# Tokens as the stationary operand for sixteen columns, and a rearranged hand-over to the last stage

## The chip, the cores and the metric

The kernel runs on one core of one Trainium2 chip. The metric is device time in microseconds (us), the median of several executions; here three executions of the kernel before gave 1936.08, 1943.45 and 1945.98 us. One further execution was recorded by the hardware profiler, and all views of the trace come from that one.

The engines of a core run side by side, each through its own list of instructions in order: PE multiplies matrices, DVE (VectorE) and ACT (ScalarE) do elementwise work and read PSUM, where PE leaves its results, POOL (GpSimd) does elementwise work on SBUF alone, and SP issues the transfers.

## The reference

One layer of a hybrid encoder, over 2048 prompt tokens and 32 sample tokens of width 1024:

```
h = layer_norm(x, ln0_g, ln0_b)
qa, ka, va, za, qkv_b, zb, a_b, b_b, gate_a, gate_b = split(h @ w_in)   # 6160 columns; a_b, b_b have 8 each
oa = chunk_band_attention(qa, ka, va, rel_bias)                  # branch A
q, k, v = silu(causal_conv(qkv_b, conv_w))                       # branch B
g    = -exp(a_log) * softplus(a_b + dt_bias)                     # decay
beta = sigmoid(b_b)
ob = rms_norm(gated_delta_rule(q, k, v, g, beta))
ya = (oa * silu(za)) @ w_branch_a;  yb = (ob * silu(zb)) @ w_branch_b
mix = sigmoid(gate_a) * ya + sigmoid(gate_b) * yb
y = layer_norm(ALPHA * h + mix @ w_out, ln_g, ln_b)              # ALPHA = 2 ** 0.25
```

## The kernel before, in words

**Stages.** The tokens go in two halves (1024, and 1024 + 32). For each half a phase B (delta rule) and then a phase A (attention) run, and under both, all the time, the input projection: 48 jobs of 128 columns of `w_in` and one job "ab" with the 8 + 8 columns of decay and beta. Sixteen jobs of a half are the merge gates; they feed nothing in the phases and serve as filling for PE. When phase A of the second half ends, the last stage ("merge") multiplies the mixed branches by `w_out`, adds the residual, normalises and stores.

**A job.** `fetch` loads 128 columns into one of two places `wraw`; `divide` finds their scale in the first half (ACT squares and sums them, PE sums over the partitions with a matmul by the tile `tiny`, `power` turns the sum into a power of two on DVE, POOL and DVE), scales them on ACT and splits them into two f16 parts, `whi` by ACT and `wlo` by POOL. `multiply` runs blocks of up to 512 tokens. Weights are the stationary operand, tokens (`hi`, `lo`, the two f16 parts of h) the moving one, so a block of 512 tokens is 8 x 3 matmuls of 128x512 into one of two PSUM banks `pj`. The job ab puts its columns' low parts beside the high ones in the same 128 columns of `whi`, and so needs 8 x 2 matmuls a block; ACT reads one group of result rows, DVE adds the other, and tokens lie along the free dimension from the start.

**The order of the work.** `Flow` is a planner that runs while the program is built: every step is a small generator, it is given a time by assumed prices, and instructions are recorded in the order of these times. All instructions of an engine thus stand in one fixed list. `HEAD` and `TAIL` are the numbers of gate jobs per half ahead of the job ab, and between the phase-B jobs and the phase-A jobs; what is left of the sixteen comes after the phase-A jobs. Since the recording goes through one helper, nearly every instruction has line L276 in the profile; L301 is a plain transfer, L312 a transposing one.

**The hand-over to the merge.** `early` multiplies the branch outputs (`ghi`, `glo`) by `w_a` or `w_b` ahead of the merge and stores the products (`sg`, later `sl`) in the buffers `sig` in DRAM. In the merge, `load` brings two of them back as `sf`, `fold` adds them (DVE) and rounds them on ACT to `mh`, the rest being `ml`. `w_out` has eight row blocks k = 0 to 7; `load_o` loads k = 0 to 3 through the places `wraw` into the space that the tokens had, after both `h_free` gates are open, that is after the last job's first and last block. Then the front space is given free (`front_done`) and `last_weights` loads the rows `l0g` and `l0b`, multiplies both by ALPHA on ACT, then loads k = 4 to 7 as halves `wr` and `lnb`. `x_ahead` loads the inputs again as `xt` and rebuilds the residual from them with `l0g` and `l0b`.

## Time and profile before

| what | value |
|---|---|
| median of three executions | 1943.45 us (1936.08 to 1945.98) |
| the profiled execution, its own time | 1944.59 us |
| its span, first to last instruction | 1942.5 us |
| granted TensorE clock, mean | 0.987 |
| PE busy | 1863.8 us, 96% |
| DVE, ACT, POOL busy | 1392.5, 987.7, 812.0 us |
| moved by transfers | 274.51 MB, 141 GB/s over the span |

A busy PE is the union of its matmuls' modelled times, and matmuls overlap; what one costs in a stream is the distance from start to start, which the timeline gives. In the timeline, the columns are start, duration, engine, line, operation and its operands, and in brackets the idle time just before it with what ended it. Landmarks of the span: the first attention scores of the first half start at 533.9 us, the job ab of the second half at 798.0, the last scores at 1657.9, the merge at 1698.6.

### The profile page before, as it was taken

How to read it: one execution, taken by the hardware profiler on the slowest of the kernel's cores; microseconds unless marked ns; L12 is line 12 of the kernel's file. 1: busy time of each engine (PE TensorE's matmuls, PEld its weight loads, DVE VectorE, ACT ScalarE, POOL GpSimd, SP SyncE). 2: the span in 40 equal slices, each digit the busy share in tenths (PEclk: the TensorE clock that was granted, in tenths of full speed). 3: DMA queues.
4: the chain of work that ended last, by engine and by line, in shares of the span. 5: the costliest groups of instructions: out<-in, count | busy, mean ns of one | idle time of the engine just before them, and what ended most of it. 6: DMA issues, size and time to landing. Idle time of an engine off the chain costs nothing.

```text
span 1942.5 us, 39504 instructions
## 1 busy us (share of the span) xinstructions
PE 1863.8 (96%) x13812; PEld 1296.6 (67%) x13812; DVE 1392.5 (72%) x4248; ACT 987.7 (51%) x2010; POOL 812.0 (42%) x1165
## 2 busy tenths in 40 slices
PE   8999999999999999999999999999999999899998
PEld 5445666767454556666778768767778667678886
DVE  7689997973377778679998986365456565475797
ACT  6665545444486878564545443355446574321110
POOL 7354445443443435355344443423222242253673
PEclk8999999999999999999999999999999999999999
DMA  3224342242468887222233242478778798995552
GB/s 134 72 90 111 78 110 80 76 110 82 124 160 188 186 188 176 68 82 71 67 96 103 61 109 72 134 209 207 215 181 200 180 200 202 260 329 190 182 184 88
DMA packets 382943, 274.51 MB, mean 141 GB/s; under 512 B 248338, under 2 KB 319358, under 8 KB 382744
## 3 DMA queue, kind: packets, MB, share of 16 engines
q1 hardware_dynamic: 382744, 272.00, 52.7%
q8 instruction: 108, 1.77, 0.4%
q14 instruction: 91, 0.75, 0.1%
HBM read 157.15 MB, written 71.76 MB: 118 GB/s over the span
## 4 chain that ended last, share of the span: by engine, by line
PE 67%; DVE 18%; issue 4%; DMA 4%; ACT 4%; POOL 2%; SPq 1%; POOLq 0%; DVEq 0%; ACTq 0%
PE pj L276 39%; PE b L276 10%; PE a L276 6%; DVE sys_u L276 4%; PE x L276 3%; PE c L276 3%; DVE acc L276 2%; PE d L276 2%; PE o L276 2%; DVE sys_t L276 2%; POOL wlo L276 1%; DVE v_t L276 1%; SPq L301 1%; DVE st L276 1%; ACT whi L276 1%
## 5 line engine op out<-in xcount | busy, mean ns | idle before, releaser
L276 PE MATMUL pj<-hi,whi 128*128 128x512 f16 (+2 forms) x1992 | 644.6, 339 | 10.1 <-ACT part L276 2.3
L276 PE MATMUL pj<-hi,wlo 128*128 128x512 f16 (+2 forms) x1952 | 636.4, 339 | 1.1 <-POOL wlo L276 1.0
L276 PEld LDWEIGHTS <-whi 128*128 128x128 f16 x3984 | 404.5, 103 | 241.9 <-issue 14.9
L276 PE MATMUL pj<-lo,whi 128*128 128x512 f16 (+2 forms) x1992 | 449.5, 338 | 0.0
L276 POOL TENSOR_TENSOR wlo<-wraw,whi 128x256 f16<-128x256 f32 (+1 forms) x392 | 281.8, 741 | 360.8 <-ACT whi L276 321.6
L276 PEld LDWEIGHTS <-wlo 128*128 128x128 f16 x1952 | 200.8, 103 | 129.0 <-issue 16.6
L276 POOL TENSOR_TENSOR pu<-sb,pu 128x640 f16<-128x640 f32 (+2 forms) x64 | 81.8, 1278 | 177.8 <-ACT pu L276 142.2
L276 ACT ACTIVATE wraw<-wraw,w_scale 128x1024 f32<-128x1024 f32 (+1 forms) x98 | 111.3, 1136 | 73.2 <-DVE w_scale L276 70.8
L276 ACT CAST whi<-wraw 128x512 f16<-128x512 f32 (+2 forms) x212 | 128.0, 611 | 38.4 <-PE pj L276 35.2
L276 ACT ACTIVATE sb<-sb,mx,unit 128x640 f32<-128x640 f32 (+4 forms) x128 | 108.6, 849 | 69.5 <-DVE mx L276 63.3
L276 DVE SCALAR_TENSOR_TENSOR acc<-raw,cwT,acc 128x512 f32<-128x512 f32 x144 | 112.9, 784 | 8.8 <-ACT acc L276 7.6
L276 ACT CAST mh<-sf 128x256 fp32r<-128x256 f32 x64 | 25.6, 406 | 153.3 <-PE c L276 80.5
L276 DVE CUSTOM_DVE_ANT_0 sb<-a,bias 128x320 f32<-128x320 f32 (+5 forms) x136 | 66.5, 498 | 44.9 <-PE a L276 39.9
L276 DVE SCALAR_TENSOR_TENSOR sys_u<-sys_p,sys_u 128x20 f32<-128x20 f32 (+11 forms) x408 | 93.4, 275 | 3.7 <-DMA sys_p<-sol_p 1.4
L276 POOL TENSOR_TENSOR ml<-sf,mh 128x256 fp32r<-128x256 f32 x60 | 62.1, 1036 | 81.0 <-PE c L276 43.7
L276 POOL TENSOR_TENSOR st<-state,sc 128x128 f32<-128x128 f32 (+1 forms) x80 | 31.1, 388 | 142.6 <-DVE state L276 122.7
L276 DVE TENSOR_TENSOR sys_u<-sys_u,sys_t 128x60 f32<-128x60 f32 (+17 forms) x323 | 79.2, 246 | 5.7
L276 DVE SCALAR_TENSOR_TENSOR sg<-sg,b 128x512 f32<-128x512 f32 (+2 forms) x49 | 29.7, 606 | 74.5 <-PE b L276 66.1
L276 ACT CAST pu<-sb 128x640 f16<-128x640 f32 (+4 forms) x128 | 82.3, 650 | 1.4 <-DMA pt<-pu 0.8
L276 ACT ACTIVATE sig<-pj,w_both 128x512 f32<-128x512 f32 (+2 forms) x84 | 49.2, 586 | 66.2 <-PE pj L276 54.2
L276 DVE TENSOR_TENSOR sys_t<-sys_u,sys_p 128x60 f32<-128x60 f32 (+17 forms) x323 | 78.6, 244 | 5.6
L276 PEld LDWEIGHTS <-pt 128*128 128x128 f16 x1680 | 65.7, 98 | 22.6 <-issue 3.7
(390 smaller groups left out, 4045.3 us busy)
## 6 DMA issues: line engine op xcount, KB each, us to landing
wraw<-in_w_in SPq DMA_DIRECT2D x192, 256.0 KB
sf<-sig SPq DMA_DIRECT2D x112, 128.0 KB
sig<-sig SPq DMA_DIRECT2D x44, 256.0 KB
sg<-sig SPq DMA_DIRECT2D x40, 256.0 KB
sig<-sg SPq DMA_DIRECT2D x40, 256.0 KB
sys_p<-sol_p SPq DMA_DIRECT2D x68, 128.0 KB
x<-in_x_p SPq DMA_DIRECT2D x16, 512.0 KB
xt<-in_x_p SPq DMA_DIRECT2D x16, 512.0 KB
```

The lines of the kernel that those rows point to most:

```text
L276: r = f(*a, **k)
L301: eng.dma_start(dst, src)
```

## The change

1. **Job ab with tokens stationary.** The sixteen columns are loaded as one piece. `whi` holds 16 high and 16 low columns, and they move past the tokens: for each 128 tokens and each k, one matmul with `hi` stationary and 32 moving columns, and one with `lo` stationary and 16. The results have tokens on the partitions. ACT reads the low group of a block, DVE adds the high group into a tile `abt`, PE transposes it 128 tokens at a time into a bank `b`, and DVE and ACT go on from there as before.
2. **ScalarE reads the sums.** In `power`, for all but the first four jobs, the step that takes the sum out of PSUM and adds 1e-24 is an ACT instruction in place of a DVE one (45 times).
3. **One gate job moved.** `TAIL` goes from [6, 5] to [5, 5]: in the first half one gate job stands after the phase-A jobs and no longer ahead of them.
4. **Residual unscaled.** `l0g` and `l0b` are not multiplied by ALPHA any more (two ACT instructions of 128x1024 less). The product's factor becomes 0.5 / ALPHA, and LN_EPS is divided by ALPHA squared, which gives the same normalised rows.
5. **First quarter of w_out sooner.** `load_o` takes k = 0 and 1 once the first gate `h_free` is open, and k = 2 and 3 once the second is.

```diff
-HEAD, TAIL = [2, 3], [6, 5]
+HEAD, TAIL = [2, 3], [5, 5]
...
-        V.tensor_scalar(out=out, in0=ps[:, 0:1], scalar1=1e-24, scalar2=None, op0=ALU.add)
+        if len(started) > 4:
+            S.activation(out=out, in_=ps[:, 0:1], func=AF.Copy, bias=1e-24)
+        else:
+            V.tensor_scalar(out=out, in0=ps[:, 0:1], scalar1=1e-24, scalar2=None, op0=ALU.add)
...
-        for g in h_free:
-            yield g
         for i in range(2):
+            yield h_free[i]
...
-        for k in range(KO):
-            yield from load_rows(w_out, k, lambda c: [x[k][:, c * 512:(c + 1) * 512] for x in wo],
-                                 lambda c: w_ready["o", k, c])
+            for k in range(2 * i, 2 * i + 2):
+                yield from load_rows(w_out, k, lambda c, k=k: [x[k][:, c * 512:(c + 1) * 512] for x in wo],
+                                     lambda c, k=k: w_ready["o", k, c])
...
+                if job.cols < P:
...
+                    for i in range(len(tiles)):
+                        m, W = min(P, n - i * P), job.cols
+                        toks = slice(i * P, i * P + m)
+                        for k in range(KD):
+                            PE.matmul(ps[:m, i * 2 * W:(i + 1) * 2 * W], hh[:, k, toks], wh[:, k, 0:2 * W],
+                                      start=(k == 0), stop=False)
+                            PE.matmul(ps[:m, i * 2 * W:i * 2 * W + W], hl[:, k, toks], wh[:, k, 0:W],
+                                      start=False, stop=(k == KD - 1))
...
-                S.activation(out=ab[0:40], in_=ps[HD:HD + 40, 0:n], func=AF.Copy, scale=inv[HD:HD + 40])
+                V.memset(rows, 0.0)
+                S.activation(out=halves, in_=lo_, func=AF.Copy, scale=inv)
                 yield
-                V.scalar_tensor_tensor(out=ab[0:40], in0=ps[0:40, 0:n], scalar=inv[0:40], in1=ab[0:40], op0=ALU.mult,
-                                       op1=ALU.add)
+                V.scalar_tensor_tensor(out=halves, in0=hi_, scalar=inv, in1=halves, op0=ALU.mult, op1=ALU.add)
                 bank["pj"].give()
                 yield
-                V.tensor_scalar(out=ab[0:NH], in0=ab[0:NH], scalar1=dtb[:], scalar2=None, op0=ALU.add)
-                S.activation(out=ab[32:40], in_=ab[32:40], func=AF.Tanh, scale=0.5)
+                yield bank["b"]
+                ps = pt("b")
+                for i in range(nt):
+                    PE.transpose(ps[0:40, i * P:i * P + m], rows[:, i, 0:40], ident[:m, :m])
+                yield
+                V.tensor_scalar(out=ab[0:NH], in0=ps[0:NH, 0:n], scalar1=dtb[:], scalar2=None, op0=ALU.add)
+                S.activation(out=ab[32:40], in_=ps[32:40, 0:n], func=AF.Tanh, scale=0.5)
+                bank["b"].give()
...
-            S.activation(out=r, in_=r, func=AF.Copy, scale=ALPHA)
...
-            V.scalar_tensor_tensor(out=xt[:rows, cs], in0=part, scalar=0.5, in1=xt[:rows, cs],
+            V.scalar_tensor_tensor(out=xt[:rows, cs], in0=part, scalar=0.5 / ALPHA, in1=xt[:rows, cs],
```

**How the order moves.** Three places show it; names are those of the program, with the buffers' numbers partly left out.

PE, second half, the end of the job ab and the first matmuls of the next job. Before:

```order
L276 LDWEIGHTS whi
L276 MATMUL pj<-lo_9305,whi 128x32
L276 LDWEIGHTS whi
L276 MATMUL pj<-lo_9305,whi 128x32
L276 LDWEIGHTS whi
L276 MATMUL pj<-hi_9018,whi 128x512
L276 LDWEIGHTS wlo
L276 MATMUL pj<-hi_9018,wlo 128x512
L276 LDWEIGHTS whi
```

After:

```order
L276 LDWEIGHTS lo_9437
L276 MATMUL pj<-whi,lo_9437 32x16
L276 LDWEIGHTS hi_9436
L276 MATMUL pj<-whi,hi_9436 32x32
L276 LDWEIGHTS lo_9437
L276 MATMUL pj<-whi,lo_9437 32x16
L276 MATMUL b<-ident,abt 40x128 x8
L276 LDWEIGHTS whi
L276 MATMUL pj<-hi_9221,whi 128x512
```

The job now ends with 32-token blocks whose stationary operand is the tokens, and the eight transposes of its two 512-token blocks stand ahead of the next job's first matmul. They read `abt`, which ACT and DVE write from PSUM first.

ACT, first half, one weight job between the squares (`whi,w_sq<-wraw`) and the scaling (`wraw<-wraw,w_scale`). Before:

```order
L276 ACTIVATE whi,w_sq<-wraw_145 128x1024
L276 ACTIVATE sig<-pj,w_both 128x512
L276 COPY u_bd_747<-tu 32x8x32 x4
L276 ACTIVATE wraw_145<-wraw_145,w_scale 128x1024
L276 CAST whi<-wraw_145 128x512
L276 COPY z_c<-d 32x256 x2
```

After:

```order
L276 ACTIVATE whi,w_sq<-wraw_145 128x1024
L276 ACTIVATE sig<-pj,w_both 128x512
L276 COPY v_t_765<-o 128x64
L276 COPY v_t_763<-o 128x64
L276 ACTIVATE w_scale<-b 128x1
L276 ACTIVATE wraw_145<-wraw_145,w_scale 128x1024
```

The reading of the sum, `w_scale<-b`, stands on ACT's own list now, ahead of the scaling.

SP, around the start of the merge: `wraw<-in_w_out` are two of the row blocks k = 0 to 3, `l0g` the first row of `last_weights`, `sf` the merge's first operands, `glo`, `sl` and `sg` the operands and results of `early`. Before, the last of k = 0 to 3, then the merge's first transfers:

```order
L301 DMA wraw_146<-in_w_out 128x1024
L301 DMA ga_15851<-za_91 128x256
L301 DMA sig_71<-sg 128x512
L301 DMA g_66<-ga_15850 128x256
L301 DMA sig_72<-sg 128x512
L301 DMA sg<-sig_74 128x512
L301 DMA sig_73<-sg 128x512
L301 DMA g_66<-ga_15851 128x256
L301 DMA sg<-sig_75 128x512
L301 DMA l0g<-in_ln_g 128x1024
L301 DMA sf<-sig_68 128x256
L301 DMA sf<-sig_76 128x256
```

After, the merge's first transfer, and then the place where k = 2 and 3 stand:

```order
L301 DMA sig_73<-sg 128x512
L301 DMA sg<-sig_75 128x512
L301 DMA g_66<-ga_16109 128x256
L301 DMA sig_74<-sig 128x272
L301 DMA sf<-sig_68 128x256
L301 DMA sf<-sig_76 128x256
```

```order
L301 DMA glo<-g_66 128x4x256 x2
L301 DMA sl<-sig_68 128x512
L301 DMA sl<-sig_69 128x512
L301 DMA sl<-sig_70 128x512
L301 DMA sl<-sig_71 128x512
L301 DMA sl<-sig_72 128x512
L301 DMA sl<-sig_73 128x512
L301 DMA sig_75<-sg 128x512
L301 DMA wraw_145<-in_w_out 128x1024
L301 DMA wraw_146<-in_w_out 128x1024
L301 DMA sig_75<-sig 128x272
```

Before, k = 0 to 3 all stand ahead of the first `sf`, with `l0g` between. Now k = 0 and 1 stand 26 rows ahead of it, k = 2 and 3 stand 19 rows behind it, `l0g` 36 rows behind it, and the halves of k = 4 to 7 stand 44 to 77 rows behind it (12 to 35 before).

More of the change, by code (lines that the diff above doesn't have):

```diff
@@ L716, in divide @@
                 yield
-                rest_ = lo[:, ks] if job.cols == P else hi[:, ks, job.cols:P]
+                rest_ = lo[:, ks] if job.cols == P else hi[:, ks, job.cols:2 * job.cols]
                 for q in range(0, 4, 2):
@@ L762, in multiply @@
                 ps = pt("pj")
+                if job.cols < P:
+                    for i in tiles:
+                        yield l_ready[job.half][i]
+                    for i in range(len(tiles)):
[6 more added lines that the diff above has]
+                                      start=False, stop=(k == KD - 1))
+                            if k % 4 == 3:
+                                yield
+                    if bi == len(job.blocks) - 1 and not job.own:
+                        w_gate.give()
+                    flow.start(evac(job, bi, c0, n, gcol, ps))
+                    continue
                 for k in range(KD):
@@ L765, in multiply @@
                     yield
-                    if job.cols == P:
-                        PE.matmul(ps[:, 0:n], wl[:, k], hh[:, k, :], start=False, stop=False)
-                        yield
+                    PE.matmul(ps[:, 0:n], wl[:, k], hh[:, k, :], start=False, stop=False)
+                    yield
                 for i in tiles:
@@ L1002, in evac @@
                 ab = raw[:, c0:c0 + n] if bi < 2 else raw_s[:, 0:n]
-                inv = w_inv[:, 48:49]
-                S.activation(out=ab[0:40], in_=ps[HD:HD + 40, 0:n], func=AF.Copy, scale=inv[HD:HD + 40])
+                m, nt = min(n, P), (n + P - 1) // P
+                inv = w_inv[:m, 48:49]
+                rows = bp.tile([P, 8, 32], F32, tag=("tu", "tu_t", "z_c")[bi], bufs=1, name="abt")
+                rows = rows[:].rearrange("p (t a) r -> p t (a r)", a=2)[:m, 0:nt]
+                halves = rows.rearrange("p t (g r) -> p t g r", r=32)[:, :, :, 0:NH]
+                hi_, lo_ = (ps[:m, 0:nt * 32].rearrange("p (t w g r) -> w p t g r", w=2, g=2, r=NH)[w] for w in range(2))
+                V.memset(rows, 0.0)
+                S.activation(out=halves, in_=lo_, func=AF.Copy, scale=inv)
                 yield
-                V.scalar_tensor_tensor(out=ab[0:40], in0=ps[0:40, 0:n], scalar=inv[0:40], in1=ab[0:40], op0=ALU.mult,
-                                       op1=ALU.add)
+                V.scalar_tensor_tensor(out=halves, in0=hi_, scalar=inv, in1=halves, op0=ALU.mult, op1=ALU.add)
                 bank["pj"].give()
                 yield
-                V.tensor_scalar(out=ab[0:NH], in0=ab[0:NH], scalar1=dtb[:], scalar2=None, op0=ALU.add)
-                S.activation(out=ab[32:40], in_=ab[32:40], func=AF.Tanh, scale=0.5)
+                yield bank["b"]
+                ps = pt("b")
+                for i in range(nt):
+                    PE.transpose(ps[0:40, i * P:i * P + m], rows[:, i, 0:40], ident[:m, :m])
+                yield
+                V.tensor_scalar(out=ab[0:NH], in0=ps[0:NH, 0:n], scalar1=dtb[:], scalar2=None, op0=ALU.add)
+                S.activation(out=ab[32:40], in_=ps[32:40, 0:n], func=AF.Tanh, scale=0.5)
+                bank["b"].give()
                 yield
@@ L2139, in all_jobs @@
                 elif what == "ab":
-                    yield Job(half, 48, [(0, w_ab[:, :, 0:NH]), (32, w_ab[:, :, NH:2 * NH])], key=(1, None, 0), cols=HD,
-                              blocks=AB_BLOCKS[half])
+                    yield Job(half, 48, [(0, w_ab)], key=(1, None, 0), cols=2 * NH, blocks=AB_BLOCKS[half])
                 else:
@@ L2198, in row, with landed @@
             t = dma(rowv[name][:], src.rearrange("(o d) -> o d", o=1).to_broadcast([P, D]))
-            if name[0:2] == "l0":
-                flow.start(scale(rowv[name][:], t, name == "l0b"))
+            if name == "l0b":
+                flow.start(landed(t))
             yield t - LEAD
-        def scale(r, t, last):
+        def landed(t):
             yield t
-            S.activation(out=r, in_=r, func=AF.Copy, scale=ALPHA)
-            if last:
-                rows_ready.done()
+            rows_ready.done()
         for name, src in (("l0g", ln0_g), ("l0b", ln0_b)):
@@ L2501, in finish @@
         V.bn_aggr(out=m2[:rows], in_=w.st[:rows])
-        V.tensor_scalar(out=m2[:rows, 1:2], in0=m2[:rows, 1:2], scalar1=LN_EPS, scalar2=None, op0=ALU.add)
+        V.tensor_scalar(out=m2[:rows, 1:2], in0=m2[:rows, 1:2], scalar1=LN_EPS / ALPHA ** 2, scalar2=None, op0=ALU.add)
         yield
```

## The prediction

> **What bounds the kernel now.** I read the page first (share of each engine, then the forty slices), then the waits of PE, then PE's timeline at each place where the change touches it.
>
> ```profile
> PE 1863.8 (96%) x13812; PEld 1296.6 (67%) x13812; DVE 1392.5 (72%) x4248; ACT 987.7 (51%) x2010; POOL 812.0 (42%) x1165
> PE   8999999999999999999999999999999999899998
> ```
>
> PE is full in all slices, and no stage has another bound. So time is won only as PE work removed or PE waits removed; work of other engines counts only where PE waits for it. The largest single wait of PE, and those of the job ab:
>
> ```profile
> PE a L276 <- ACT mh L276: 8.0, 1, 8.0
> ...
> PE pj L276 <- DVE ab L276: 1.5, 1, 1.5
> ...
> PE b L276 <- DVE ab L276: 1.2, 1, 1.2
> ```
>
> The first is the hand-over to the merge. The many others are below 5 us in sum each.
>
> **Edit 1, job ab.** PE's timeline of the job in both halves (first row: its start; 65.30: the next job):
>
> ```profile
> 58.36 1.89 PE L276 MATMUL pj<-hi,whi 128*128 128x512 f16 x8
> ...
> 65.30 0.38 PE L276 MATMUL pj<-hi,whi 128*128 128x512 f16 x1
> ...
> 798.02 1.89 PE L276 MATMUL pj<-hi,whi 128*128 128x512 f16 x8
> ...
> 804.92 0.35 PE L276 MATMUL pj<-hi,whi 128*128 128x32 f16 x8
> 805.13 0.35 PE L276 MATMUL pj<-lo,whi 128*128 128x32 f16 x8
> 807.03 0.38 PE L276 MATMUL pj<-hi,whi 128*128 128x512 f16 x1 [1.55 <-DVE ab L276]
> ...
> 812.96 1.13 PE L276 MATMUL b<-ident,ab 40*64 40x40 f32 x32 [1.24 <-DVE ab L276]
> ```
>
> Removed: 65.30 - 58.36 = 6.9 us, and 798.02 to about 805.3 = 7.3; together 14.2. Added: 128 small matmuls in the first half and 144 in the second, 272, each with its own stationary operand. The nearest rows are the 32-token block above (stationary 128x128, 32 columns moving: eight in 805.13 - 804.92 = 0.21 us, 26 ns each) and the attention's `c`, which also changes its stationary operand every time:
>
> ```profile
> 1675.64 0.61 PE L276 MATMUL c<-vt,pt 128*128 128x64 f16 x15 [1.68 <-DMA pt<-pu]
> 1676.09 0.47 PE L276 MATMUL pj<-ghi,whi 128*128 128x512 f32 x1
> ...
> 42.74 0.60 PE L276 MATMUL a<-ident,x 128*128 128x128 f32 x4
> 43.18 0.27 PE L276 MATMUL pj<-hi,whi 128*128 128x256 f16 x1
> ...
> L276 PEld LDWEIGHTS <-pt 128*128 128x128 f16 x1680 | 65.7, 98 | 22.6 <-issue 3.7
> ```
>
> Fifteen in 0.45 us are 30 ns. At 28 ns, between the two, 272 cost 7.6 us. The 17 transposes cost 0.44 / 4 = 0.11 us each, 1.9 in all. Sum: 7.6 + 1.9 - 14.2 = **-4.7 us** (-5.2 at 26 ns, -4.1 at 30). The upper bound is a load that nothing hides, 98 ns by the last row: a rival below.
>
> The waits around it change their cause. Before, PE waited 1.55 us for DVE to empty a bank. Now the eight transposes stand on PE ahead of the next job's matmuls, behind the same two readers:
>
> ```profile
> 805.12 0.68 ACT L276 ACTIVATE ab<-pj,w_both 40x512 f32<-40x512 f32 x1 [1.27 <-PE pj L276]
> ...
> 804.24 0.91 DVE L276 MEMSET q_bd<- 128x1024 f32 x1 [0.16 <-issue]
> ...
> 806.90 0.23 DVE L276 SCALAR_TENSOR_TENSOR ab_s<-pj,w_both,ab_s 40x32 f32<-40x32 f32 x1
> ```
>
> The new readers handle 64 elements a partition for 512, about 0.3 us each by the last row, but may stand behind a clearing of 0.9: PE waits 1 to 2 us, as before. All of the next job is queued behind. The later wait of 1.24 has some ten us of matmuls ahead of it now and should go; I take -1 for it (0 to -3, since the clock after it was halved for some us, below).
>
> **Edits 2 and 3.** What moves from DVE, and the nearest small reading of PSUM on ACT:
>
> ```profile
> L276 DVE TENSOR_SCALAR w_scale<-b x49: 106/157/160, 15.5 to 725.0; 128x1 f32<-128x1 f32 x49
> ...
>   ACT wraw L276: 70.8, 38
> ...
> L276 ACT COPY v_t<-o 128x64 f32<-128x64 f32 x132 | 26.4, 212 | 99.8 <-PE o L276 77.8 <-DVE state L276 17.8 <-DVE ms L276 2.4
> ```
>
> 45 x 0.16 = 7 us leave DVE and 45 x 0.2 = 9 us go to ACT, over 700 us in which neither bounds. The new wait: ACT stands in its list until PE has done the small sum, and everything queued on ACT (a `sig`, a `v_t`, the scaling) waits with it. But ACT already stood 70.8 us, 38 times, for the end of this chain, so the wait mostly moves. What hides it is the second pair of weight buffers. If that cover is gone, 45 x 0.05 = 2 us reach PE. A shorter list on DVE, for which PE waits most often, can give some back. Together -0.5 (-4 to +3).
> The Trainium skill speaks against it: "ScalarE: Activation LUTs", Rules for kernel authors, gives adds and multiplies to VectorE; at the 187 ns that its section on ACT_TABLE_LOAD yields, 45 x 0.03 = 1.4 us would be lost, an estimate.
> The gate job is the same PE work 250 us later. Cover is lost at the end of phase B (where jobs of the same kind follow) and gained at the end of phase A: 0 (-3 to +3). The new order reshuffles some 50 us of small waits: 0 (-5 to +5).
>
> **Edits 4 and 5, the hand-over.** Timelines of SP, DVE, ACT and PE, then the windows (PE, PEld, DVE, ACT, POOL busy, clock, DMA share, GB/s):
>
> ```profile
> 1688.53 0.38 SPq L301 DMA_DIRECT2D l0g<-in_ln_g  x1
> ...
> 1695.95 0.42 DVE L276 TENSOR_TENSOR sf<-sf 128x256 f32<-128x256 f32 x1 [1.91 <-DMA sf<-sig]
> ...
> 1694.69 1.06 ACT L276 ACTIVATE l0g<-l0g 128x1024 f32<-128x1024 f32 x1 [8.51 <-DMA l0g<-in_ln_g]
> 1697.22 1.06 ACT L276 ACTIVATE l0b<-l0b 128x1024 f32<-128x1024 f32 x1 [1.48 <-DMA l0b<-in_ln_b]
> 1698.19 0.39 ACT L276 CAST mh<-sf 128x256 fp32r<-128x256 f32 x1
> ...
> 1689.56 1.08 PE L276 MATMUL pj<-glo,whi 128*128 128x512 f32 x4
> 1698.63 0.79 PE L276 MATMUL a<-wohi,mh 128*128 128x512 f32 x1 [7.99 <-ACT mh L276]
> ...
> 1700.07 0.63 PE L276 MATMUL a<-wolo,mh 128*128 128x512 f32 x1
> 1700.50 0.63 PE L276 MATMUL a<-wohi,mh 128*128 128x512 f32 x1
> ...
> 1702.84 0.39 PE L276 MATMUL a<-wohi,mh 128*128 128x512 f32 x1
> 1703.07 0.40 PE L276 MATMUL a<-wolo,mh 128*128 128x512 f32 x1
> ...
> 1724.69 0.62 ACT L276 CAST woh<-lnb 128x512 fp32r<-128x512 f32 x1 [0.99 <-DMA lnb<-in_w_out]
> ...
> 1690.00:1699.00 9.00, 1.01 (x4) 0.56 (x3) 1.75 (x5) 2.41 (x3) 0.00 (x0) 0.76 0.94 294
> 1699.00:1726.00 27.00, 27.00 (x112) 21.72 (x112) 20.08 (x28) 10.58 (x25) 15.97 (x15) 0.95 0.98 333
> 1726.00:1760.00 34.00, 31.92 (x157) 25.29 (x155) 27.61 (x41) 5.82 (x16) 20.55 (x20) 1.00 0.86 287
> ```
>
> The sum `sf` is ready at 1696.4, but the cast to `mh` stands on ACT behind the two scalings, until 1698.2. Edit 4 ends those 1.8 us. The rest is landing time: 512 KB of `l0g` ahead. And the wait cost more than 8.0: the clock is 0.76 there, and PE's first seven merge matmuls take 0.43 us from start to start, later 0.23; 1.5 us more. The place costs **9.5 us**.
>
> The pace of blocks of 272 columns:
>
> ```profile
> 820.52 0.28 PE L276 MATMUL pj<-hi,whi 128*128 128x272 f16 x1
> 820.64 0.28 PE L276 MATMUL pj<-hi,wlo 128*128 128x272 f16 x1
> ```
>
> After, call T the issue of the first transfer of the hand-over. The store `sig_74` just ahead of it comes after the last block but one; behind that PE has 24 matmuls of 272 columns (0.12 each) and 24 of 512 (0.23): 8.4 us, less 1.2 for ACT's read. So PE has work until T + 7.2 (T + 2.1 before), and `mh` is there by about T + 6.5. The first wait is gone.
> What is late next: `w_out`. Before, 0.5 MB were in at T + 6.2 (`l0g`) and the 10.2 MB up to the last `lnb` at T + 36.2, that is 323 GB/s, at a DMA share of 0.94 and more. Counting the sizes in SP's new order with this rate, both parts of `glo` (2.6 MB) are in at T + 12.7, k = 2 (5.0 MB) at T + 20, the second half of k = 4 (12.7 MB) at T + 44, `glo` of the next 256 tokens (13.8) at T + 47.2, the last half of k = 7 (17.9) at T + 60. PE does k = 0 and 1 (24 matmuls, 5.6 us) until T + 12.8, waits for `glo` with its casts until 14.7, does four products of `early` (48 matmuls, 11.2 us), k = 2 with four more (14), k = 3 (2.8) and the start of k = 4, until T + 43.2; it waits for the second half of k = 4 until 45.5, ends k = 4 at 47.8, waits for `glo` until 49.2. From there the smaller products fill up to k = 7. That is 5.6 us of waits and, with a half clock, about 6.6 in place of 9.5: **-3 us** (-9.5 if transfers run better, +4 if `ghi`, `mh` and `wohi` hold each other up on ACT). Nothing else follows from the sooner quarter: k = 0 and 1 were in time before.
>
> **Sum.** -4.7 - 1 - 0.5 - 3 = -9.2. The profiled execution took 1944.59 us, so **1935 us**. The median is 1.1 below that execution, so against it this is 8 us, 0.4%. A measurement here tells about 0.5% (9.7 us) from no change.
>
> **Rivals.**
> *The hand-over is won whole.* For it: 1726 to 1760 runs at 287 GB/s without PE starving, so the products can bridge. Against it: the 0.98 share. 9.5 in place of 3: 1929 us.
> *The gains are eaten.* ACT and DVE hold the transposes in both halves (2 us each), the order's small waits rise by 4: 1943 us.
> *w_out starves the merge, slower than before.* k = 2 to 7 now stand behind the products' traffic on SP, whose list also waits for DVE and ACT. If SP's stalls bring the rate to 230 GB/s, the second half of k = 4 comes 15 us later (12.2 MB / 0.23 against / 0.323) and the waits sum to about 27 with the half clock: +18 - 6 = +12, 1957 us. By the same count the hand-over wins nothing below some 300 GB/s, and below about 260 the whole change is slower. Against it: 294 to 333 in the windows.
> *The stationary loads don't overlap.* 272 x 98 ns = 26.7 us, +14.4 in place of -4.7: 1954 us. The rows of 26 and 30 ns speak against it.
> The Trainium skill has that rule: "TensorE: Matmul & The Clock Gate", LDWEIGHTS, puts a load at its columns over 1.2 GHz, 107 ns, which would make 29 us of the 272, an estimate. The trace disagrees wherever loads follow each other.
>
> **How the numbers follow.** Forecast 0.45 (its own range 1929 to 1942), whole hand-over 0.28, eaten 0.12, starved 0.11, loads 0.04. Faster by over 0.5% is nearly all of the second and a third of the first: 0.42. Slower: most of the last two, 0.12. The rest, 0.46, is within. The range 1925 to 1950 leaves out the far ends of the second and most of the slow cases.
>
> **What would show it.** Job ab: 272 rows `pj<-hi` with 32 and 16 columns, 26 to 30 ns from start to start; a wait of 1 to 2 us before `b<-ident,abt`. Hand-over: no 8 us ahead of the first `a<-wohi`, but waits ahead of a `pj<-ghi` and of `woh` (k = 4) that sum to 4 to 8. PE's busy time some 5 us lower. Wrong, if the waits behind the first `a<-wohi` exceed 10 us, if none is there at all, or if a wait of the phases before, which I put at zero, moved the time by more than 5.

## The result

Over ten executions each, the changed kernel takes 1926.79 us (1922.31 to 1936.11) and the kernel before 1940.88 us (1936.08 to 1945.98). The ratio is 0.9929, with a 95% interval of 0.9915 to 0.9944: faster by 0.7%, some 14 us, where 8 were forecast against the median shown. One execution of all those told of here, of `quarter_alone` below, took 2325 us at a mean granted clock of 0.75 and is left out of its ratio, clock loss and remainder. The profiled execution of the changed kernel took 1929.68 us, with a span of 1927.9. Against the span before that is 14.6 us less, and this is what the pieces below have to add up to.

Two rows of the profile page of the changed kernel, PE's busy time with its instructions, and its forty slices:

```profile
PE 1854.3 (96%) x14021; PEld 1298.4 (67%) x14021; DVE 1390.9 (72%) x4208; ACT 989.3 (51%) x2053; POOL 810.2 (42%) x1165
...
PE   8998999999999998999999999999999999999998
```

PE still sets the time; the hollow slice of the hand-over (an 8 late in the row before) is gone, and two slices of the first half show an 8 where a 9 stood. Stage by stage, from the windows view. The stages are: from the first matmul of the job ab to the same job of the second half, on to the first `a<-wohi` of the merge, on to the end. The columns are length, busy time of PE, PEld, DVE, ACT and POOL, granted clock, DMA share, GB/s. Before:

```profile
58.40:798.00 739.60, 713.50 (x5262) 435.53 (x5261) 552.44 (x1868) 450.20 (x873) 319.11 (x496) 0.99 0.49 122
798.00:1698.60 900.60, 867.32 (x7190) 641.08 (x7187) 616.59 (x2006) 465.26 (x967) 325.44 (x493) 0.99 0.57 144
1698.60:1942.50 243.90, 233.65 (x1088) 190.75 (x1088) 182.66 (x249) 36.05 (x95) 128.84 (x125) 0.98 0.59 195
```

After:

```profile
58.20:799.80 741.60, 710.35 (x5368) 436.22 (x5367) 549.32 (x1826) 454.72 (x918) 326.42 (x497) 1.00 0.47 121
799.80:1681.80 882.00, 861.07 (x7295) 641.43 (x7292) 614.85 (x2006) 460.32 (x962) 316.17 (x490) 1.00 0.56 145
1681.80:1927.90 246.10, 233.81 (x1088) 191.62 (x1088) 185.37 (x250) 38.62 (x99) 129.80 (x127) 0.98 0.60 200
```

The first half became 2.0 us longer, though PE has less to do in it, the second half 18.6 shorter, the merge 2.2 longer. I split every stage into three: the idle times in brackets of PE's rows (waits), half of the busy time that the trace records at half clock (half clock), and the rest, which is work. By this split the 14.6 us are:

| piece | us |
|---|---|
| work of PE, 3.7 of it in the two halves | -4.7 |
| wait at the hand-over, 7.99 to 0.92 | -7.1 |
| waits and half clock later in the merge | +3.1 |
| other waits of the second half, 24.8 to 19.3 | -5.5 |
| half clock of the second half, 8.5 to 3.4 | -5.1 |
| waits of the first half, 24.9 to 31.0 | +6.1 |
| half clock of the first half, 4.8 to 3.4 | -1.4 |

The first three are what edits 1, 4 and 5 were summed for, without the waits around the job ab: -8.7, against a forecast of -4.7 - 3 = -7.7. The other four, -5.9, stand in the two phases. Two parts of them belong to edits: the waits around the second job ab went from 1.55 + 1.24 to 1.01 + 1.19 us (-0.6, forecast -1), and a wait of 1.68 us at 1675.64, in a row that the prediction shows, is gone; the runs below trace it to edit 5. What is left, -3.6, stands at places that edits 1, 4 and 5 do not touch; the forecast had -0.5 for edits 2 and 3 and zero for the order.

The job ab in the changed kernel, PE's timeline (start, duration, instruction, and in brackets the idle time ahead of it):

```profile
58.24 0.18 PE L276 MATMUL pj<-whi,hi 128*128 128x32 f16 x1
58.27 0.17 PE L276 MATMUL pj<-whi,lo 128*128 128x16 f16 x1
...
61.44 0.16 PE L276 MATMUL b<-w_sq,tiny 128*128 128x1 bf16 x1
61.47 0.38 PE L276 MATMUL pj<-hi,whi 128*128 128x512 f16 x1
61.68 0.60 PE L276 MATMUL b<-ident,abt 128*40 128x128 f32 x4
62.11 0.38 PE L276 MATMUL pj<-hi,wlo 128*128 128x512 f16 x1
...
799.75 0.18 PE L276 MATMUL pj<-whi,hi 128*128 128x32 f16 x1
...
803.52 1.05 PE L276 MATMUL b<-ident,abt 128*40 128x128 f32 x8
804.41 0.38 PE L276 MATMUL pj<-hi,whi 128*128 128x512 f16 x1
...
806.23 0.18 PE L276 MATMUL b<-ident,abt 32*40 32x32 f32 x1 [1.01 <-DVE abt L276]
...
815.37 0.84 PE L276 MATMUL b<-ident,ab 40*64 40x40 f32 x22 [1.19 <-DVE ab L276]
```

The 128 small matmuls of the first half take 61.44 - 58.24 = 3.20 us, 25 ns each; the 144 of the second 803.52 - 799.75 = 3.77 us, 26 ns. Four transposes take 62.11 - 61.68 = 0.43. A wait ahead of the next job's first matmul is gone; 1.01 us stands ahead of the last transpose and 1.19 ahead of `b<-ident,ab`.

The hand-over in the changed kernel, timelines of SP, ACT and PE:

```profile
1673.52 1.38 SPq L301 DMA_DIRECT2D sf<-sig  x3
...
1681.36 0.70 ACT L276 CAST mh<-sf 128x256 fp32r<-128x256 f32 x2
...
1718.23 0.62 ACT L276 CAST woh<-wr 128x512 fp32r<-128x512 f32 x1 [3.19 <-DMA wr<-in_w_out]
...
1679.80 1.09 PE L276 MATMUL pj<-lo,whi 128*128 128x272 f16 x8
1681.81 0.50 PE L276 MATMUL a<-wohi,mh 128*128 128x512 f32 x1 [0.92 <-ACT mh L276]
...
1718.90 0.79 PE L276 MATMUL a<-woh,mh 128*128 128x512 f32 x1 [2.99 <-ACT woh L276]
1720.64 0.79 PE L276 MATMUL a<-wol,mh 128*128 128x512 f32 x1 [0.95 <-POOL wol L276]
...
1724.64 0.41 PE L276 MATMUL pj<-ghi,whi 128*128 128x256 f32 x1
```

With T = 1673.52, PE has work until 1681.81 - 0.92 = T + 7.4, and the next wait is the second half of k = 4 of `w_out`, over at T + 45.4. The twelve matmuls from 1718.90 to 1724.64 take 5.74 - 0.95 = 4.79 us at a halved clock, 2.0 more than twelve of 0.23. The place costs 0.92 + 2.99 + 0.95 + 2.0 = 6.9 us; it was 9.5.

### The profile page after: what moved, and what is told of

It is laid out like the page before. It is cut to its first block, busy times and chain, and to the rows that moved or that the text cites. A ratio compares the mean times of both kernels' runs of the same rounds, so it can differ in the third digit from the quotient of the medians.

```text
span 1927.9 us, 39964 instructions
## 1 busy us (share of the span) xinstructions
PE 1854.3 (96%) x14021; PEld 1298.4 (67%) x14021; DVE 1390.9 (72%) x4208; ACT 989.3 (51%) x2053; POOL 810.2 (42%) x1165
## 5 line engine op out<-in xcount | busy, mean ns | idle before, releaser
L276 PE MATMUL pj<-hi,whi 128*128 128x512 f16 (+2 forms) x1952 | 632.0, 338 | 11.5 <-ACT vf L276 4.3
L276 PEld LDWEIGHTS <-whi 128*128 128x128 f16 x3904 | 396.2, 103 | 230.9 <-issue 12.3
L276 POOL TENSOR_TENSOR wlo<-wraw,whi 128x256 f16<-128x256 f32 (+1 forms) x392 | 285.9, 752 | 366.1 <-ACT whi L276 310.1
L276 PE MATMUL pj<-lo,whi 128*128 128x512 f16 (+2 forms) x1952 | 438.9, 338 | 0.0
L276 ACT ACTIVATE wraw<-wraw,w_scale 128x1024 f32<-128x1024 f32 (+1 forms) x98 | 110.7, 1130 | 59.0 <-DVE w_scale L276 57.8
L276 DVE SCALAR_TENSOR_TENSOR sg<-sg,b 128x512 f32<-128x512 f32 (+2 forms) x56 | 34.5, 615 | 80.1 <-PE b L276 74.8
L276 PE MATMUL b<-ghi,whi 128*128 128x512 f32 (+2 forms) x224 | 85.7, 390 | 1.0 <-DVE cr L276 1.0
L276 POOL TENSOR_TENSOR w_scale<-w_scale,mhalf 128x1 f32<-128x1 f32 x49 | 32.0, 652 | 126.3 <-ACT w_scale L276 118.3
```

The lines of the kernel that those rows point to most:

```text
L276: r = f(*a, **k)
```

## The experiments

All ratios are against the kernel before, which ran beside each of them on the same chip (medians of 1940 to 1941 us). Each execution lists its span and mean granted clock; "clock loss" is span x (1 - clock), and "remainder" is the time without it, both as means over all executions of the kernel. It counts half clock while PE waits too, so it bounds from above what half clock costs. The ratio is an estimate from executions that ran side by side; it differs from the quotient of the medians by up to 0.0011. "First half" and "second half" are waits + half clock of the profiled execution, by the split above, with the first wait of the merge inside the second half.

| kernel | edits | median us | ratio (95%) | clock loss | remainder | first half | second half | first wait of the merge |
|---|---|---|---|---|---|---|---|---|
| before | none | 1940 to 1941 | 1 | 19.2 to 20.2 | 1920.5 to 1921.4 | 24.9 + 4.8 | 32.8 + 8.5 | 7.99 |
| after | 1 to 5 | 1926.79 | 0.9929 (0.9915, 0.9944) | 14.1 | 1913.2 | 31.0 + 3.4 | 20.2 + 3.4 | 0.92 |
| ab_alone | 1 | 1947.95 | 1.0045 (1.0029, 1.0060) | 28.6 | 1920.5 | 34.4 + 18.3 | 28.8 + 6.5 | 7.40, ahead of `pj<-ghi` |
| power_alone | 2 | 1957.41 | 1.0085 (1.0063, 1.0106) | 28.0 | 1928.6 | 34.6 + 10.8 | 35.4 + 4.8 | 9.10 |
| tail_alone | 3 | 1946.43 | 1.0038 (1.0023, 1.0052) | 25.3 | 1921.5 | 29.2 + 7.6 | 31.6 + 8.5 | 7.39 |
| resid_alone | 4 | 1941.00 | 1.0003 (0.9991, 1.0015) | 20.7 | 1920.7 | 23.6 + 5.1 | 30.7 + 6.8 | 6.16 |
| quarter_alone | 5 | 1934.48 | 0.9968 (0.9953, 0.9982) | 16.2 | 1918.1 | 23.8 + 4.8 | 27.7 + 6.8 | 5.75 |
| hand_alone | 4, 5 | 1933.85 | 0.9968 (0.9954, 0.9982) | 15.8 | 1918.1 | 23.9 + 4.8 | 25.9 + 5.0 | 3.91 |
| null_spread | none, another order | 1948.38 | 1.0042 (1.0027, 1.0056) | 24.2 | 1924.0 | 30.2 + 7.9 | 31.6 + 1.7 | 8.16 |
| after_null | 1 to 5, another order | 1936.29 | 0.9973 (0.9960, 0.9985) | 21.4 | 1914.0 | 34.7 + 11.3 | 19.9 + 3.4 | 0.92 |
| no_ab | 2 to 5 | 1940.17 | 0.9996 (0.9983, 1.0009) | 17.4 | 1921.7 | 31.8 + 10.1 | 22.3 + 3.2 | 0.92 |
| no_power | 1, 3 to 5 | 1942.05 | 1.0015 (1.0001, 1.0029) | 25.8 | 1917.0 | 32.4 + 19.3 | 22.2 + 0.0 | 0.92 |
| no_tail | 1, 2, 4, 5 | 1934.21 | 0.9968 (0.9956, 0.9980) | 16.3 | 1917.3 | 35.5 + 3.4 | 23.7 + 0.0 | 0.92 |
| after_k4 | 1 to 5, k = 4 sooner | 1935.66 | 0.9975 (0.9959, 0.9991) | 16.9 | 1918.0 | 30.6 + 1.7 | 20.9 + 0.0 | 0.92 |

### ab_alone: edit 1 alone

The kernel before with the job ab of the change and nothing else.

```diff
+                if job.cols < P:
...
+                            PE.matmul(ps[:m, i * 2 * W:(i + 1) * 2 * W], hh[:, k, toks], wh[:, k, 0:2 * W],
+                                      start=(k == 0), stop=False)
```

> The kernel before with edit 1 alone (job ab with tokens stationary). Sum of parts: 272 small matmuls at 25 ns and 17 transposes at 0.11 us in place of 14.2 us, so 5 us less PE work, and the new list of every engine adds or takes small waits of PE, -5 to +5: ratio 0.995 to 1.000, likeliest 0.9975. Rival, that this edit alone makes the whole gain, since the earlier bank and the later transposes also take waits out of the second half: ratio 0.993.

Measured: 1947.95 us, ratio 1.0045. Alone, the job with less work makes the kernel slower. That is outside the 0.995 to 1.000 that was expected, and on the other side from the rival. PE's work in the first half did fall, to 706.2 us by the split, from 710.0 before. But the planner gave the two phases another order: first-half waits went from 24.9 to 34.4 us and half clock from 4.8 to 18.3. In the means, all of the loss is clock (28.6 for 19.3); the remainder is that of before, so the longer waits took back what the work saved. The saving is there, and a worse order ate it.

### resid_alone and hand_alone: edit 4, and edits 4 and 5

The kernel before with the unscaled residual, and with the sooner quarter as well. Both keep the phases' order of before.

```diff
-            V.scalar_tensor_tensor(out=xt[:rows, cs], in0=part, scalar=0.5, in1=xt[:rows, cs],
+            V.scalar_tensor_tensor(out=xt[:rows, cs], in0=part, scalar=0.5 / ALPHA, in1=xt[:rows, cs],
```

> The kernel before with edit 4 alone (l0g and l0b not scaled); SP's list stays the same. Sum of parts: the first cast mh no longer stands behind two ACT instructions that wait for landings, so the 8.0 us wait at the start of the merge shrinks by 1.8 us to about 6.2, and up to 1 us of half clock with it; nothing else moves: ratio 0.9985 to 0.9995. Rival, that the wait is of landings alone: the wait stays at 8, ratio 1.000.

> The kernel before with edits 4 and 5 (first quarter of w_out sooner); k = 2 and 3 then also stand ahead of the first sf, and lists differ only around the hand-over. Sum of parts: what edit 4 gives, and nothing from edit 5, as k = 0 to 3 were in time: first wait of the merge about 6, ratio 0.998 to 0.9995. Rival, that the sooner quarter empties the transfers' backlog ahead of l0g and sf, so that they land sooner: first wait of the merge 4 or less, ratio 0.996.

Measured: edit 4 alone cannot be told from no change (1.0003); both together are worth 0.32%. The first wait of the merge, PE's timeline of `resid_alone` and then `hand_alone`:

```profile
1692.72 0.79 PE L276 MATMUL a<-wohi,mh 128*128 128x512 f32 x1 [6.16 <-ACT mh L276]
...
1685.85 0.50 PE L276 MATMUL a<-wohi,mh 128*128 128x512 f32 x1 [3.91 <-ACT mh L276]
```

Edit 4 took 7.99 - 6.16 = 1.8 us from the wait, as the prediction said. That the median does not show it is no contradiction: its interval reaches 1.7 us to the fast side. With edit 5 another 2.25 us go (6.16 - 3.91), for which the prediction had no step; the rival named for `hand_alone`, a wait of 4 or less, is what came.

### quarter_alone: edit 5 alone

```diff
         for i in range(2):
+            yield h_free[i]
...
-        for k in range(KO):
+            for k in range(2 * i, 2 * i + 2):
```

> The kernel before with edit 5 alone (k = 0 and 1 of w_out once the first gate is open). The list of the two phases is that of before, so only the last 260 us can differ. Theory A (the sooner quarter is what shortened the first wait of the merge when edits 4 and 5 stood together, since 4 MB fewer stand ahead of l0g and sf): the wait ahead of the first a<-wohi falls from 8.0 to 5 to 6 us, the scaling of l0g on ACT still stands ahead of mh; 3 to 5 us won, ratio 0.997 to 0.999. Rival B (edit 5 pays only with the two scalings gone, because mh stands on ACT behind l0b): the wait stays at 7 to 8, ratio 0.999 to 1.001.

Measured: 1934.48 us, ratio 0.9968, and a wait of 5.75 us: the sooner quarter pays by itself, so the expectation that it needs edit 4 falls. (The expectation's 4 MB is a slip; the sooner quarter is two row blocks of 0.5 MB.) The gains add up: 7.99 - 1.83 - 2.24 = 3.92, and both edits together show 3.91. What the traces show behind it, first in `before`: DVE's timeline, then SP's waits from 1682 to 1689:

```profile
1685.91 1.58 DVE L276 TENSOR_TENSOR wolo<-wraw,wohi 128x512 fp32r<-128x512 f32 x2
1689.56 0.69 DVE L276 SCALAR_TENSOR_TENSOR sg<-sg,pj 128x512 f32<-128x512 f32 x1 [2.06 <-DMA sg<-sig]
...
SPq L301 <- DMA sig<-sg: 3.4, 1, 3.4
```

And in `quarter_alone`: the same work on DVE, SP's waits from 1676 to 1681.5, `l0g` on SP and ACT, and PE's wait:

```profile
1670.88 1.28 DVE L276 TENSOR_TENSOR wolo<-wraw,wohi 128x512 fp32r<-128x512 f32 x2
1681.85 0.69 DVE L276 SCALAR_TENSOR_TENSOR sg<-sg,pj 128x512 f32<-128x512 f32 x1 [1.91 <-PE pj L276]
...
SPq L301 <- DVE sg L276: 3.5, 2, 1.9
...
1680.92 0.43 SPq L301 DMA_DIRECT2D l0g<-in_ln_g  x1
...
1686.43 1.06 ACT L276 ACTIVATE l0g<-l0g 128x1024 f32<-128x1024 f32 x1 [17.25 <-DMA l0g<-in_ln_g]
...
1690.34 0.79 PE L276 MATMUL a<-wohi,mh 128*128 128x512 f32 x1 [5.75 <-ACT mh L276]
```

Before, the last two row blocks of the first four came while `early` was still storing and reloading its products. SP stood 3.4 us for a product's store to land, and a sum `sg` on DVE waited for its reload. Sooner, all four are through, and SP waits for DVE alone, which follows PE. `l0g` now lands 5.5 us after its issue, where it took 6.2. PE's last work before the wait ends 3.7 us after that issue (1690.34 - 5.75 - 1680.92), where it was 2.1. These 0.7 and 1.6 are the 2.2 us that the wait lost. That the row blocks held the products up is read from these rows and was not tried by itself.

A second wait goes with it. In the prediction's row at 1675.64 PE waits 1.68 us for a transposing transfer (`pt<-pu`) in the phase; `resid_alone`, without edit 5, still has it:

```profile
1671.56 0.61 PE L276 MATMUL c<-vt,pt 128*128 128x64 f16 x15 [1.52 <-DMA pt<-pu]
```

In the last 80 us ahead of the merge, none of the eight kernels with edit 5 has a wait of PE over 0.3 us but the merge's first one; of the six without it, all but `ab_alone` have one of 1.3 to 1.7 there, ahead of `c<-vt,pt`. So edit 5 took 2.24 + 1.68 = 3.9 us of waits, and the second half is 6.0 us shorter in `quarter_alone` than before.

### null_spread and after_null: another order, the same work

One of the planner's numbers, the distance between eight loads at the start, is 20.4 for 20; nothing of the work changes. `null_spread` is the kernel before with it, `after_null` the changed one.

```diff
-SPREAD = 20.0
+SPREAD = 20.4
```

> The kernel before with no change of work: the planner's spacing of eight early loads of the bias rows is 20.4 instead of 20.0, which by itself gives all engines another order from there on (as many lines of PE's list differ as with any of the edits). Theory of the order's lottery, that any new order changes PE's small waits and the half-clock windows by several us: span differs by 3 to 8 us from before, either way, with the same PE work. Rival, that the order before is as good as any and such waits are alike: within 2 us, ratio 0.999 to 1.001.

> The changed kernel with no change of work: spacing of the early bias loads 20.4 instead of 20.0, another order on all engines. The changed kernel has some 6 us less of small waits and half clock outside the hand-over than the kernel before. If that is the luck of one order, as the same step cost the kernel before 8 us: slower than the changed kernel by 4 to 10 us, ratio to before 0.996 to 1.000. Rival, that edits 2 and 3 take these waits out whatever the order: ratio 0.991 to 0.995.

Measured: 1.0042 and 0.9973. A change of order that is worth nothing in work costs the kernel before 8 us. PE's list in `null_spread` is that of before up to 265 us, and from the job ab on it gets there in the same time (207.1 us, 207.3 before), so the eight loads themselves cost nothing. The changed kernel stands 8.5 us higher with the new order (0.9973 against 0.9929, intervals apart), but the two were timed in different sets, and `after_k4` below, with PE's list of the changed kernel up to 1724 us, came out 7.6 higher as well; so these 8.5 are not shown to be the order's. Under the same number the two kernels stand at 1948.38 and 1936.29, 12 us apart, about the 14 of the original pair. In the traces the waits and half clock of the first half go from 29.7 to 38.1 us and from 34.4 to 46.0. In `null_spread` the second half gives as much back (41.3 to 33.3): its profiled execution took 1945.12 us, and the one of before 1944.59, so the 8 us of the medians are not in this pair of traces.

### power_alone and tail_alone: edits 2 and 3 alone

```diff
+        if len(started) > 4:
+            S.activation(out=out, in_=ps[:, 0:1], func=AF.Copy, bias=1e-24)
...
-HEAD, TAIL = [2, 3], [6, 5]
+HEAD, TAIL = [2, 3], [5, 5]
```

> The kernel before with edit 2 alone (ScalarE reads the sums, 45 times). Same PE work. Lottery theory: any ratio from 0.996 to 1.005. Rival, that it takes out waits for good: first half's waits and half clock fall by 4 us or more against before and against the reordered kernel before, ratio 0.993 to 0.998.

> The kernel before with edit 3 alone (one gate job moved behind the phase-A jobs). Same PE work. Lottery theory: any ratio from 0.996 to 1.005. Rival, that the filling at the end of the first half's phase A takes its waits there (4 us between 745 and 775 us in before): these waits fall below 1.5 us, ratio 0.996 to 0.998.

Measured: 1.0085 and 1.0038, slower by 16 and by 7 us; the first lies outside the 0.996 to 1.005 that was expected of the order, and both rivals fail. For neither does the place of the edit explain it: the first half's waits are 10 and 4 us longer, and clock loss is 8 and 5 us more. Between 745 and 775 us, where edit 3 was to bring the waits below 1.5, they are 4.4 us, for 3.9 before. One place in `power_alone` shows a wait and half clock together, the row of the wait and then three windows around it:

```profile
615.49 0.62 PE L276 MATMUL c<-vt,pt 128*128 128x64 f16 x9 [2.22 <-DMA pt<-pu]
...
605.00:615.60 10.60, 7.57 (x64) 4.19 (x62) 8.80 (x29) 5.08 (x14) 3.86 (x6) 1.00 1.06 268
615.60:625.80 10.20, 5.10 (x40) 2.80 (x39) 9.42 (x29) 7.25 (x13) 7.81 (x9) 0.50 0.66 147
625.80:636.00 10.20, 10.20 (x75) 5.60 (x74) 8.70 (x28) 6.92 (x14) 1.10 (x2) 1.00 1.03 220
```

About 3 us of waits (2.22 here, 0.81 just before) end, and for the next 10.2 us the clock is 0.50. PE is busy for 5.10 us of them; another 5.1 are waits, 3.92 in one piece. By the split the half clock costs 2.6 us here. Not every wait does it; the changed kernel at 385 us has 1.70 in one piece, and the clock stays:

```profile
385.02 0.46 PE L276 MATMUL d<-qk,k_bd 128*128 128x128 f32 x2 [1.70 <-DVE qk_bd L276]
...
385.00:395.20 10.20, 10.18 (x65) 6.13 (x66) 7.59 (x31) 5.66 (x11) 2.29 (x3) 1.00 0.43 99
```

### no_ab, no_power, no_tail: the change without one edit

Each takes one edit back to the form of before.

> The changed kernel without edit 1 (job ab as before). PE work rises by 4 to 5 us. If work counts: slower than the changed kernel by 4 to 5 us, plus or minus 8 for the new order, ratio to before 0.992 to 0.999. Rival, that edit 1 is worth nothing or less, as it was slower alone: ratio to before at or below 0.991.

> The changed kernel without edit 2: DVE takes the weights' sums out of PSUM again, 45 times. Theory A (edit 2 has no effect of its own; alone it came out 0.85% slower since it gave the phases another order): the ratio to before lies anywhere between 0.990 and 1.000, with the waits of the first half between 34 and 46 us, as in the other orders, and PE's work by stage as in the changed kernel to 2 us. Rival B (edit 2 costs PE what it cost alone, since ACT now stands in its list): without it the kernel is over 8 us faster than the changed one, ratio below 0.989. Rival C (it is what makes the change faster): ratio over 1.000.

> The changed kernel without edit 3: TAIL is [6, 5] again. Theory A (order alone): ratio to before between 0.990 and 1.000; the waits of the first half between 34 and 46 us; PE's work of the whole span as in the changed kernel to 2 us. Rival B (the moved gate job covers waits at the end of phase B or of phase A in itself): the difference to the changed kernel stands in the last 100 us of phase B and the last 100 of phase A of the first half, and nowhere else.

Measured: 0.9996, 1.0015 and 0.9968, each slower than the whole change in its own set; `no_ab`, expected at 0.992 to 0.999, lies just above. Removing edit 2 costs 17 us (1.0015 against 0.9929), and adding it alone cost 16: its sign turns with its company. Against `after_k4`, timed in the same set, `no_power` is 8 us slower and `no_tail` is not slower (means of 1942.7 and 1933.7 us, for 1934.9), so an effect of edit 3 is not shown. The expectation that the order alone would leave `no_power` between 0.990 and 1.000, with 34 to 46 us of first-half waits, was too narrow (51.7); the one over 1.000 came out by its number. What it says, that edit 2 is what makes the change faster, cannot be the whole of it, since the same edit alone did the opposite. The excess over the changed kernel is in one stage, the first of the windows view of `no_power`:

```profile
57.10:814.50 757.40, 724.17 (x5366) 443.51 (x5365) 555.16 (x1871) 450.10 (x873) 326.56 (x497) 0.97 0.47 119
814.50:1696.00 881.50, 858.73 (x7295) 639.42 (x7294) 615.29 (x2006) 460.52 (x962) 318.41 (x490) 1.00 0.57 145
```

That stage is 15.8 us longer than in the changed kernel, at a clock of 0.97 for 1.00; its waits are nearly the same in sum, 32.4 and 31.0. So it is almost all clock, at nine places from 103 to 765 us. `no_tail` differs by 5.8 us in the first half (4.5 of waits, 1.3 of work) and by 1.1 in the second half. Of the 4.5, 2.8 stand between 550 and 700 us, where 9.5 us of waits, 6.30 of them in one row, replace 6.7, and 1.5 behind 750; so it is not only at the two ends that rival B names. Its whole work is 3.7 us more than the changed kernel's by the split, where 2 had been expected; since the split takes all half clock at full price, I read it to no better than 4 us over a whole span.

The work alone is steadier by stage. In the first half it is 706.6 us on average in the six kernels with edit 1 (standard deviation 1.3), and 709.6 in the eight without it (0.5): 3.0 us. In the second half 858.9 in the five with edit 1 (`ab_alone`, whose merge starts at another place in the order, is left out) and 860.1 in the eight: 1.2 us. Together 4.2 us, whatever the order.

### after_k4: k = 4 of w_out ahead of the residual's rows

The changed kernel, with both halves of k = 4 loaded ahead of `l0g`, `l0b` and the inputs for the residual. The lists of the phases are the same.

```diff
-        for name, src in (("l0g", ln0_g), ("l0b", ln0_b)):
-            yield from row(name, src)
-        flow.start(x_ahead())
...
+            if i == 2 * KO + 2:
+                for name, src in (("l0g", ln0_g), ("l0b", ln0_b)):
+                    yield from row(name, src)
+                flow.start(x_ahead())
```

> The changed kernel with both halves of k = 4 of w_out loaded ahead of l0g, l0b and the residual's inputs; the phases keep their list. Theory A (what is late after the hand-over is k = 4 of w_out, as the prediction counted): the waits ahead of woh and wol of k = 4 near 1719 us (2.99 and 0.95 in the changed kernel) go, with the 2.2 us of half clock behind them, and the span is 4 to 6 us shorter than the changed kernel's, ratio to before 0.990. Rival B (SP is behind as a whole, so that what is moved back is late in its turn): the same 4 to 6 us come back ahead of pj<-ghi, of k = 5 or of the first residual, ratio 0.993.

Measured: 1935.66 us, ratio 0.9975: nothing won. PE's timeline shows where the wait went:

```profile
1713.17 0.39 PE L276 MATMUL a<-woh,mh 128*128 128x512 f32 x1
1713.40 0.39 PE L276 MATMUL a<-wol,mh 128*128 128x512 f32 x1
1717.13 0.79 PE L276 MATMUL a<-woh,mh 128*128 128x512 f32 x1 [3.34 <-ACT woh L276]
```

k = 4 is in time, and the second half of k = 5 is late by 3.34 us in its place. Rival B was right on the place. The size of the ratio fits neither: its profiled execution took 1926.76 us, no slower than the changed kernel, but it is the fastest of twelve, and their means stand 7.6 us above those of the changed kernel, 2.8 of it clock loss. In the traces its merge is 1.9 us longer (248.0 for 246.1). The two were timed in different sets, and PE's list is the same up to 1724 us, while the kernel before agrees in all sets to 1 us in its remainder. I cannot say what the other 4.8 are. A difference of 7.6 us between kernels of different sets is thus not safe, and the 0.7% of the changed kernel rests on one set.

No kernel tried beats the changed one.

## Why the prediction was right, and where it was not

**The time** of 1926.8 us lies in the range of 1925 to 1950, 2 us below the forecast's own 1929 to 1942. Faster by over 0.5% had a chance of 0.42, a little less than the 0.46 for a change too small to tell. Of the 14.6 us in the profiled pair, PE's work gave -4.7 (forecast -4.7), the waits around the job ab -0.6 (-1), the hand-over with the merge behind it -4.0 (-3), the wait at 1675.64 -1.7 (0), and all else -3.6 (-0.5). The sum of the edits was nearly right; the terms for the order and for the rest of edit 5 were mis-sized.

**Edit 1: right.** 25 to 26 ns for a small matmul, where 28 was taken; 7.0 us added for 272, and 1.9 for 17 transposes. With 14.2 removed this is -5.3, where -4.7 was forecast, and the work by stage shows -4.2. PE's busy time fell by 9.5 us, where some 5 were forecast; most of the rest is less half clock, which counts as busy. The stationary loads do overlap (each is recorded at 0.10 us, and the next starts 25 ns behind it), so that rival is out. The Trainium skill, "TensorE: Matmul & The Clock Gate", Back-to-back issue gap, names an issue floor near 25 ns for up to 64 columns moving, which the rows bear out; its 81 ns for a sustained pair of load and matmul is given for 128 columns moving and has no counterpart in these rows. Of the waits around the job, the one of 1 to 2 us was put ahead of all eight transposes; 1.01 us stands ahead of the last transpose alone. The later one, put at going, stayed at 1.19; that the way through `abt`, the transposes and `b` is longer would explain it, but was not tried.

**Edits 2 and 3: the local price lies in its range, the time of the edit does not.** The tile view of `w_scale` and the waits in the changed kernel:

```profile
L276 ACT ACTIVATE w_scale<-b x45: 149/171/172, 61.8 to 729.3; 128x1 f32<-128x1 f32 x45
...
  ACT wraw L276: 57.8, 40
...
PE b L276 <- ACT w_scale L276: 3.0, 2, 1.9
```

ACT takes 0.17 us for one read and stands 57.8 us for the end of the chain, where it was 70.8; PE has a new wait of 3.0. That is the upper end of the -0.5 (-4 to +3); what DVE's shorter list gives back is not told apart. But the edit alone moved the time by +16 us and its removal by +17, and neither is in that range.

**The step that failed** is "The new order reshuffles some 50 us of small waits: 0 (-5 to +5)". Its width was too small. In the profiled pair the order, with edits 2 and 3, gave -3.6, which lies inside. But with no change of work another order cost the kernel before 8 us, and edits 2 and 3, alone, 16 and 7. All four reorderings of the kernel before (`ab_alone`, `power_alone`, `tail_alone`, `null_spread`) came out slower, so a centre of zero is not shown either, and that the whole change drew a gain is, as far as the runs show, luck. Two things were missed. The kernel before has by far the fewest first-half waits of the orders with another list of the phases (24.9, against 29 to 36), so nearly any edit that reorders loses some there. And a wait can bring a half clock that costs as much again, which the prediction had counted at the hand-over and behind one wait of the job ab only. Why one order draws more half clock than another stays open. The prediction named the sign of this: it called itself wrong if a wait of the phases, put at zero, moved the time by over 5; the first half's waits, in sum, did (+6.1).

**Edits 4 and 5: right in size, with one wrong sentence.** PE has work until T + 7.4 (forecast 7.2); `mh` is there at T + 8.2 for T + 6.5, hence the 0.92. The wait for the second half of k = 4 ends at T + 45.4 (forecast 45.5), but it is 3.9 us for 2.3, and the two for `glo`, 3.3 in sum, are not there. The place costs 6.9 us, forecast 6.6; that the sums agree so well is luck, since its parts do not. "Edit 4 ends those 1.8 us" held: 1.83. "Nothing else follows from the sooner quarter: k = 0 and 1 were in time before" was wrong: edit 5 alone took 2.24 us of this wait and the 1.68 at 1675.64, by the traces because the row blocks got out of the way of other transfers. On the list of before, edits 4 and 5 bring the wait to 3.91; in every kernel with both and at least two of the other edits it is 0.92, since there `sf` is loaded ahead of `l0g`. It does not hang on edit 1: `no_ab` has this order without it, and `ab_alone` with it alone. Which edit tips it was not tried further.

**The rivals.** "The hand-over is won whole" gave 1929 us, nearest to the measured time, but it is not what happened: the place still costs 6.9 us. "w_out starves the merge" was right about what is late and wrong by far on the size. "The gains are eaten" is what happens to edits 1, 2 and 3 alone. Two readings were too kind to PE: three of the forty slices show an 8, and in the window from 1726 to 1760, called free of starving, PE is busy for 31.92 of 34.00 us.

**By the edits, the time does not add up.** Alone they come to +0.45, +0.85, +0.38 and -0.32% (4 and 5 together), in sum +1.4%; the whole is -0.7%. And with any of the first three taken out, the kernel stands 0.4 to 0.9% above the whole, of which up to 0.46% may be the set, as `after_k4` shows. In a kernel whose order is planned anew for each edit, a run with one edit measures that edit and a draw of the order, and here the draw is the larger. That edits 1, 2 and 3 help only together, for a reason of their own, is a rival that these runs do not rule out.

## What to carry to other kernels

Where a planner sets the order, run the same kernel in another order first, at no change of work: what that moves (8 us here) is what a single edit must beat before its time says anything about it. Read an edit's worth from the work by stage and from the one wait that it touches, which came out alike wherever the list allows the comparison (4.2 us of work in all orders; 1.83 and 2.24 us that add up on the list of before), and time the whole beside its parts in one set before an edit is kept or dropped. A load moved earlier can pay by what it gets out of the way of, not only by being there sooner.

## What the runs showed of the hardware

The spread between executions of one kernel is mostly the clock. In the last set, 35 executions of the kernel before go from 1933.82 us at a mean granted clock of 0.993 to 1946.73 at 0.986; a clock lower by 0.007 over 1940 us is 13.6 us, and the times differ by 12.9. Over the 35, time and clock loss go together with a correlation of 0.86. The same list thus loses more or less clock from one execution to the next: `resid_alone` has PE's list of the kernel before throughout, and between 850 and 1650 us its trace shows half clock at 1122.7 and 1590.3 us, the other at 919.9, 991.6 and 1162.2. Over the kernels the mean clock loss goes from 14 to 29 us.

The fourteen traces have 109 stretches of half clock ahead of PE's last instruction: 67 of 3.4 us, 37 of 6.8, four of 10.2 and one of 13.7. Most stand behind or inside waits of PE, in the phases from some 0.6 us up to the 6.30 of `no_tail`. But seven have less than 0.35 us of idle PE in the 6.8 us ahead of them. All seven stand behind a run of small matmuls, of 32x32 or of two columns, in which PE counts as busy. Two windows of `tail_alone`, ahead of such a stretch and in it (PE's columns, with 6.80 busy of 6.80, come first, the clock third from the end):

```profile
1124.40:1131.20 6.80, 6.80 (x83) 4.44 (x81) 6.10 (x28) 5.98 (x14) 4.23 (x4) 1.00 0.14 50
1131.20:1138.00 6.80, 6.80 (x55) 5.33 (x52) 5.04 (x17) 2.25 (x4) 6.55 (x17) 0.50 0.31 94
```

That the small matmuls bring it is not shown; `resid_alone` halves behind the same matmuls at 1122.7, and the kernel before, with the same list, does not.

The Trainium skill, "TensorE: Matmul & The Clock Gate", HAM oscillation, sets the bound at idle gaps of more than about 3.4 us. The trace of the kernel before disagrees: only one wait of PE in it is longer than 3.4 us, the 7.99 of the hand-over, and eight of its ten stretches of half clock stand neither there nor behind the end of the work. What the Trainium skill says on the same page of a free-running window (What's actually happening) would fit a list that draws half clock in one execution and not in another; no run here tests it.
